# Rows beyond 128 of two expert blocks turned as one tile of 128 rows, and other short operands padded to 128

## The chip, the cores and the metric

One core of a Trainium2 chip runs the whole program. Its engines are TensorE (PE in the profile, with its weight loads shown apart as PEld), VectorE (DVE), ScalarE (ACT), GpSimd (POOL) and SyncE (SP), which here only issues transfers. The metric is the device time of one execution in microseconds (us). Three runs stand for the kernel before, and one more execution was profiled.

## What is computed

One layer of a hybrid trunk over 1024 tokens of width 1024: an mLSTM mixer, a residual layer norm, a mixture of 16 experts of which each token takes two, a second residual layer norm, and a gated embedding. The part around the change is the router and the experts:

```python
t = x.reshape(-1, d)                                    # 1024 tokens
scores = jax.nn.softmax((t @ router_w), axis=-1)        # 16 experts
...
for e in range(N_EXPERTS):
    h = jax.nn.silu(t @ w_gate[e]) * (t @ w_up[e])      # 1024 -> 512
    y = y + gate[:, e:e + 1] * (h @ w_down[e])          # 512 -> 1024
```

`gate` is zero for all but two experts of a token. The kernel therefore gathers for each expert only the tokens that chose it.

## The kernel before, in words

All large products are made of float32 operands split into a high and a low part (`split`: ACT writes the high part, DVE or POOL subtracts it for the low part), so that one product is two or three matmuls that go into the same sum.

The stages follow each other. The mixer's projections and its recurrence come first. Then a loop over eight tiles of 128 tokens (`project`, `normed`, `logits`) projects the mixer's output, adds the residual and makes the router's sums. In `logits` a first product puts high and low sums into 32 rows (`pl[:32, :128]`), DVE copies them to the tile `lt` of 32 partitions, and a second matmul of `lt` with the stacked identity `st2` adds the two halves and turns them at once (L890). The tiles 6 and 7 of this loop, the choice of the experts (`select`) and the placing of the tokens lie around the first expert block.

Then come 16 expert blocks. The experts are ordered by their number of tokens; `rank` is the place in that order, and `ORDER` alternates ranks below 8 with ranks from 8 on. A block r turns its gathered rows (`tr_full`, tile `xt`), and makes gate, up and down products for up to 128 rows. An expert of rank below 8 (even r) has up to 64 rows more, the mini part: `locate(r)` gathers them on POOL's queue into `xgm`, `turn_mini` (`tr_mini`) turns them while block r-1's up product runs, and `first_mini` makes gate and up of them, with high and low part side by side as 128 columns of one stationary tile `xm`. `fold` adds the two halves, `gated` multiplies silu(gate) by up into the tile `sg`, `tr_mini` turns the result (`hm`) between the steps of the down product, and `mini_out` makes the down product.

`turned` is the helper in which all these transposes are recorded (L446): four matmuls against the identity into one PSUM tile, then a split. With `n=64` it reads 64 partitions:

```python
PE.transpose(pt[:, k, :n], src[:n, 128 * (q + k):128 * (q + k) + 128], ident[:n, :n])
```

Block 0 is handled apart: its transposes of `xgm` stand as a group of eight, its `hm` is turned at L1293, and `fill_table` then makes for all blocks the table `tab` of token numbers by 32 small matmuls (L1196).

From the tile 6 of the projection on, the order on PE, ACT, DVE and POOL is the order in which the code is written; before it only that of PE and SP is. `run(chain, also=...)` weaves the steps of one generator between those of another, and `tick` hands out the splits of the coming expert's weights (`wraw` to `whi` and `wlo`) at fixed steps of PE's work.

Of the kernel before, what the change touches and what calls it, by code (L numbers as in the profile page):

```python
# [24 lines left out]
D = 1024  # L25
# [20 lines left out]
def trunk(ctx, tc, io, out):  # L46
# [79 lines left out]
    with ExitStack() as pa:  # L126
# [315 lines left out]
        def turned(src, q, hi, lo, n=128):  # L442

            pt = ptr.tile([128, 4, 128], F32, name="tr")
            for k in range(4):
                PE.transpose(pt[:, k, :n], src[:n, 128 * (q + k):128 * (q + k) + 128], ident[:n, :n])  # L446
            split(hi, lo, pt[:, :, :n])

# [135 lines left out]

    def gather_x(idx, n):
        xg = mt([128, D], F32, name="xg" if n == 128 else "xgm")
        G.indirect_dma_start(out=xg[:n], out_offset=None, in_=x1_d,
                             in_offset=bass.IndirectOffsetOnAxis(ap=idx[:n, :1], axis=0))
        return xg
# [11 lines left out]

    def tr_mini(res, src, nk, name):

        dst = mt([128, nk, 128], F32R, name=name, bufs=1)
        res.append(dst)
        for q in range(0, nk, 4):
            turned(src, q, dst[:, q:q + 4, :64], dst[:, q:q + 4, 64:], 64)
            yield

# [25 lines left out]

    def first_mini(res, x, w, name, late=False):
        ps = pmm.tile([128, 512], F32, name="mm")
        for k in range(ND):
            wh, wl = use(w[k // 4])
            product(ps, [(x[0][:, k], wh[:, k % 4]), (x[0][:, k], wl[:, k % 4])], k == 0, k == ND - 1)  # L640
            if k == ND - 1:
                if late:
                    yield
                dst = mt([64, DE], F32, name=name, bufs=1)
                fold(ps, dst)
                res.append(dst)
            yield
# [76 lines left out]

    FETCH, IDX, X, XM, WG, WU, WD = ({} for _ in range(7))
    mini = lambda i: ORDER[i] < NMINI
# [23 lines left out]
    def locate(r):  # L750

        e = ORDER[r]
        X[r] = gather_x(tab[:, 0, e:e + 1], 128)
        if mini(r):
            XM[r] = gather_x(tab[:, 1, e:e + 1], 64)

# [4 lines left out]
    def turn_mini(r):  # L761
        rows, XM[r] = XM[r], []
        return tr_mini(XM[r], rows, ND, "xm")

# [29 lines left out]
    with ExitStack() as pb_:  # L794
# [83 lines left out]
        def logits(t, bank=None):  # L878
# [102 lines left out]
        for t in range(NT - 1):  # L981
# [48 lines left out]
            if t < NT - 2:  # L1030
# [88 lines left out]
    with pe_:  # L1119
        PIECES[2] = [early, pe_.enter_context(pool("moew5", reuse_waits="tile"))]  # L1120
        home(pe_.enter_context(pool("moex", reuse_waits="tile")), "xg")
        home(pm_.enter_context(pool("moem", reuse_waits="tile")), "xm hm gs us fold e")
        last = NE - 1
        first_slot = lambda i: 128 * ORDER[i] + 64 * min(ORDER[i], NMINI)
# [65 lines left out]
        def fill_table():  # L1190

            pi = pix.tile([128, 512], F32, name="pi")
            for j, (a, b) in enumerate(((0, 128), (128, 192))):
                for k in range(2):
                    for c in range(NT):
                        PE.matmul(pi[:b - a, 32 * j:32 * j + 32], em[:, k, c, a:b], ids[:, k, c],  # L1196
                                  start=k + c == 0, stop=k + c == NT)
            idf = mt([128, 2, 2, NE], F32, name="idf", bufs=1)
            for j, n in enumerate((128, 64)):
                V.tensor_copy(idf[:n, j], pi[:n, 32 * j:32 * j + 32])  # L1200
                tt(tab[:n, j], idf[:n, j, 0], idf[:n, j, 1], op=ALU.add)

        V.tensor_copy(flat(prefs), prefp)
# [56 lines left out]
        ids = mt([128, 2, NT, 2, NE], BF, name="ids", tag="ht")  # L1260
        gm, chain = part(first_mini, XM[0], WG[0], "gs")
        run(chain, 5)
# [8 lines left out]
        splits(1)  # L1271
        um, chain = part(first_mini, XM[0], WU[0], "us", True)
        run(chain, 6)
# [8 lines left out]
        run(chain)  # L1282
        sg = gated(sg, um[0], 64)
        hm = sg
        fetcher(2)
# [6 lines left out]
        for k in range(4):  # L1292
            PE.transpose(pt[:, k, :64], hm[:64, 128 * k:128 * k + 128], ident[:64, :64])  # L1293
        hm32 = mt([128, NF, 128], F32, name="hm32", tag="hm", bufs=1)
# [73 lines left out]
        for r in range(1, NE):  # L1368
# [22 lines left out]
            if mini(r):  # L1391
                sg = silu(gm[0], 64)
                um, chain = part(first_mini, XM[r], WU[r], "us")
                run(chain)
                sg = gated(sg, um[0], 64)
            if r < last:
# [4 lines left out]
            if r < last:  # L1401
                g, chain = part(first_full, X[r + 1], WG[r + 1])
                if mini(r):
# [3 lines left out]
                    clock[1] = 1  # L1407
                    hm = sg
                    run(chain)
# [12 lines left out]
            if r < last and mini(r + 1):  # L1422
                gm, chain = part(first_mini, XM[r + 1], WG[r + 1], "gs")
                run(chain)
                if r + 2 < NE:
                    WG[r + 2] = fetch(r + 2, 0)
# [5 lines left out]
            if r == last:  # L1432
                WU[NE] = [queue_piece(raw_of(io["pgw"][i]), (2, D), 2, V) for i in range(2)]
                g2 = mt([128, D], F32, name="g2", tag="xgm")
# [44 lines left out]
        with tc.If(n_over > 0), tc.For_i(0, n_over):  # L1479
# [32 lines left out]
            V.tensor_copy(svb, sv)  # L1512
            e2 = mt([128, 2, NT, 128], BF, name="e2", tag="xgm")
            for k in range(2):
# [165 lines left out]
def _layout(x, p, ln1_g, ln1_b, ln2_g, ln2_b, mlstm_w_in, mlstm_conv, mlstm_gate_b, mlstm_norm_g,  # L1680
# [41 lines left out]
    d["pgw"] = c(ple_w_gate)[0].reshape(4, 2, 128, D).transpose(0, 2, 1, 3).reshape(4, 128, 2 * D)  # L1722
    d["st2"] = np.concatenate([np.eye(NE), np.eye(NE)])
    return {k: np.ascontiguousarray(v, dtype=np.float32) for k, v in d.items()}
# [15 lines left out]
```

## Time and profile before

| | |
|---|---|
| three runs | 978.39, 982.37, 984.08 us (median 982.37) |
| the profiled execution, its own time | 979.86 us |
| its span, first to last instruction | 978.2 us |
| PE busy | 959.8 us, 98% of the span |
| DVE, ACT, POOL busy | 655.0, 540.5, 249.4 us (67%, 55%, 25%) |

The span lies 1.66 us inside the profiled execution's own time. A busy PE is a PE with some matmul under way; matmuls overlap, so what one costs is read from the distance between starts. The three runs lie 5.7 us apart, which is 0.6% of the time.

### The profile page before, as it was taken

How to read it: one execution, taken by the hardware profiler on the slowest of the kernel's cores; microseconds unless marked ns; L12 is line 12 of the kernel's file. 1: busy time of each engine (PE TensorE's matmuls, PEld its weight loads, DVE VectorE, ACT ScalarE, POOL GpSimd, SP SyncE). 2: the span in 40 equal slices, each digit the busy share in tenths (PEclk: the TensorE clock that was granted, in tenths of full speed). 3: DMA queues.
4: the chain of work that ended last, by engine and by line, in shares of the span. 5: the costliest groups of instructions: out<-in, count | busy, mean ns of one | idle time of the engine just before them, and what ended most of it. 6: DMA issues, size and time to landing. Idle time of an engine off the chain costs nothing. (4 is left out here: it accounts for less than half of the span.)

```text
span 978.2 us, 14851 instructions
## 1 busy us (share of the span) xinstructions
PE 959.8 (98%) x5468; PEld 810.2 (83%) x5468; DVE 655.0 (67%) x1218; ACT 540.5 (55%) x902; POOL 249.4 (25%) x246
## 2 busy tenths in 40 slices
PE   7999999999999999998999999999999999999998
PEld 5989989899999888877668787878787878778887
DVE  5657656372443177789758779776767676688882
ACT  6336556454464255444358767676767576654441
POOL 0001212021000121111224442424242423233531
PEclk9999999999999999999999999999999999999999
DMA  8116921213336465612788988988989897764531
GB/s 314 64 51 250 331 82 55 75 49 92 97 104 202 157 237 211 234 51 104 256 297 318 329 325 293 335 332 291 335 290 341 315 347 297 271 239 147 173 108 65
DMA packets 51395, 207.03 MB, mean 212 GB/s; under 512 B 6892, under 2 KB 15724, under 8 KB 38264
## 3 DMA queue, kind: packets, MB, share of 16 engines
q1 hardware_dynamic: 43640, 182.48, 52.0%
q0 software_dynamic: 5968, 22.55, 6.9%
q10 hardware_dynamic: 1712, 1.03, 0.3%
q8 instruction: 44, 0.72, 0.3%
q14 instruction: 31, 0.25, 0.1%
HBM read 170.35 MB, written 35.68 MB: 211 GB/s over the span
## 5 line engine op out<-in xcount | busy, mean ns | idle before, releaser
L515 DVE TENSOR_TENSOR wlo<-wraw,whi 128x1024 fp32r<-128x1024 f32 x150 | 206.0, 1409 | 25.2 <-ACT whi L514 24.2
L514 ACT ACTIVATE whi<-wraw 128x1024 fp32r<-128x1024 f32 x194 | 195.1, 1051 | 9.1 <-DMA wraw<-eu 4.6
L63 PE MATMUL mm<-whi,xt 128*128 128x512 f32 (+1 forms) x528 | 168.4, 390 | 0.0
L515 POOL TENSOR_TENSOR wlo<-wraw,whi 128x1024 fp32r<-128x1024 f32 x44 | 108.8, 2481 | 224.4 <-ACT whi L514 224.3
L63 PE MATMUL mm<-wl,xh 128*128 128x256 f32 (+1 forms) x512 | 145.8, 285 | 0.0
L63 PE MATMUL mm<-wh,xh 128*128 128x256 f32 (+1 forms) x512 | 145.5, 284 | 0.0
L63 PE MATMUL mm<-wh,xl 128*128 128x256 f32 (+1 forms) x512 | 145.2, 284 | 0.0
L63 PEld LDWEIGHTS mm<-whi,xt 128*128 128x128 f32 x528 | 97.0, 188 | 21.7 <-issue 1.2
L63 PE MATMUL mm<-wlo,xt 128*128 128x512 f32 (+1 forms) x264 | 99.8, 387 | 0.9 <-DVE wlo L515 0.5
L63 PEld LDWEIGHTS mm<-wh,xh 128*128 128x128 f32 x512 | 96.8, 189 | 0.2 <-ACT sg L250 0.2
L63 PEld LDWEIGHTS mm<-wl,xh 128*128 128x128 f32 x512 | 96.8, 189 | 0.1
L63 PEld LDWEIGHTS mm<-wh,xl 128*128 128x128 f32 x512 | 96.7, 189 | 0.0
L63 PE MATMUL mm<-woh,yt 128*128 128x512 f32 x256 | 89.5, 408 | 0.3 <-ACT yt L57 0.3
L63 PE MATMUL mm<-whi,ht 128*128 128x512 f32 x240 | 86.3, 408 | 0.0
L63 PE MATMUL mm<-whi,x2t 128*128 128x512 f32 (+1 forms) x272 | 84.4, 385 | 0.0
L58 DVE TENSOR_TENSOR wl<-wr,wh 128x1024 fp32r<-128x1024 f32 (+2 forms) x26 | 29.7, 1145 | 45.4 <-ACT wh L57 45.0
L63 PEld LDWEIGHTS mm<-whi,x2t 128*128 128x128 f32 x272 | 50.1, 188 | 10.1
L63 PEld LDWEIGHTS mm<-wlo,xt 128*128 128x128 f32 x264 | 48.7, 188 | 11.0 <-DVE wlo L515 1.2
L63 PE MATMUL mm<-xh,wh 128*128 128x512 f32 x128 | 50.7, 405 | 6.9 <-ACT xh L57 6.9
L63 PEld LDWEIGHTS mm<-woh,yt 128*128 128x128 f32 x256 | 48.0, 188 | 10.7 <-ACT yt L57 0.5
L63 PEld LDWEIGHTS mm<-whi,ht 128*128 128x128 f32 x240 | 45.0, 188 | 10.6 <-DVE ht L58 0.8
L63 PE MATMUL mm<-wlo,x2t 128*128 128x512 f32 (+1 forms) x136 | 52.0, 382 | 0.0
(382 smaller groups left out, 1965.6 us busy)
## 6 DMA issues: line engine op xcount, KB each, us to landing
wraw<-eg SPq DMA_DIRECT2D x32, 1024.0 KB, 6.8
wraw<-ed SPq DMA_DIRECT2D x32, 1024.0 KB, 6.3
wraw<-eu SPq DMA_DIRECT2D x30, 1024.0 KB, 6.8
y_d<-zt SPq DMA_DIRECT2D x16, 512.0 KB, 5.6
y_d<-yo SPq DMA_DIRECT2D x14, 512.0 KB, 7.3
num_d<-nb SPq DMA_DIRECT2D x32, 128.0 KB, 1.8
wr<-wo SPq DMA_DIRECT2D x8, 512.0 KB, 4.5
sig_d<-sg SPq DMA_DIRECT2D x32, 128.0 KB, 1.8
```

The costliest lines, as they stand in the source:

```text
L58: (eng or V).tensor_tensor(lo, src, f32(hi), op=ALU.subtract)
L63: PE.matmul(ps, a, b, start=start and i == 0, stop=stop and i == n - 1)
L514: S.activation(hi[:, c], raw[:, c], AF.Copy)
L515: e.tensor_tensor(lo[:, c], raw[:, c], f32(hi)[:, c], op=ALU.subtract)
```

## The change

Mini rows of two blocks are gathered and turned together. Rows of block r (r = 2, 6, 10, 14) stand in partitions 0 to 63 of one `xgm` tile and rows of block r+2 in partitions 64 to 127 (for r = 14 the upper half holds rows that nothing uses); `tr_pair` turns them by 128-row transposes into one `xm` tile for both. `xgm` has one buffer now, and block 0 uses a first tile whose upper half is filled with zeros. The gated mini rows go into one fixed tile `us`, whose upper half is zeroed once, and are turned with 128 rows. `lt` becomes two fixed tiles of 128 partitions, zeroed but for the first 32, and `st2` has 128 rows. `fill_table` gets a third group of 16 matmuls, and one more addition on DVE, that put the table's rows for block r+2 into partitions 64 to 127.

```diff
@@ turned
             for k in range(4):
-                PE.transpose(pt[:, k, :n], src[:n, 128 * (q + k):128 * (q + k) + 128], ident[:n, :n])
-            split(hi, lo, pt[:, :, :n])
+                PE.transpose(pt[:, k], src[:, 128 * (q + k):128 * (q + k) + 128], ident)
+            split(hi, lo, pt[:, :, :n] if hi.ndim == 3 else pt.rearrange("p k (m t) -> p k m t", m=2))
...
-    def gather_x(idx, n):
-        xg = mt([128, D], F32, name="xg" if n == 128 else "xgm")
+    FIRST = []
+
+    def gather_x(idx, n, name="xg", **kw):
+        xg = FIRST.pop() if n == 64 else mt([128, D], F32, name=name, **kw)
...
+    def tr_pair(res, src):
+
+
+        dst = mt([128, ND, 2, 2, 64], F32R, name="xm", bufs=1)
+        res += [dst[:, :, i].rearrange("p k h t -> p k (h t)") for i in range(2)]
+        for q in range(0, ND, 4):
+            turned(src, q, *[dst[:, q:q + 4, :, i] for i in range(2)])
+            yield
...
-        if mini(r):
-            XM[r] = gather_x(tab[:, 1, e:e + 1], 64)
+        if r % 4 == 2:
+            XM[r] = gather_x(tab[:, 1, e:e + 1], 128, "xgm", bufs=1)
...
     def turn_mini(r):
-        rows, XM[r] = XM[r], []
-        return tr_mini(XM[r], rows, ND, "xm")
+
+        if r % 4 == 2 or r == 0:
+            pair = []
+            for j in range(2):
+                XMP[r + 2 * j] = pair, j
+            return tr_pair(pair, XM[r])
+        return iter(())
...
-        st2 = sp.tile([32, NE], F32, name="st2", bufs=1)
+        st2 = sp.tile([128, NE], F32, name="st2", bufs=1)
...
+        LT = [sp.tile([128, 128], F32, name=f"lt{i}", bufs=1) for i in range(2)]
+        for lt in LT:
+            G.memset(lt, 0.0)
...
             with tc.high_priority(offset=200):
-                lt = sp.tile([32, 128], F32, name="lt", bufs=2)
-                V.tensor_copy(lt, pl[:32, :128])
-            yield
-            PE.matmul(pl[:, 256:256 + NE], lt, st2, start=True, stop=True)
+                V.tensor_copy(LT[t % 2][:32], pl[:32, :128])
+            yield
+            PE.matmul(pl[:, 256:256 + NE], LT[t % 2], st2, start=True, stop=True)
...
+        FIRST.append(mt([128, D], F32, name="xgm", bufs=1))
+        G.memset(FIRST[0][64:], 0.0)
...
+        US = mt([128, DE], F32, name="us", bufs=1)
+        G.memset(US[64:], 0.0)
...
-            for j, (a, b) in enumerate(((0, 128), (128, 192))):
+            for j, a, b in (0, 0, 128), (1, 64, 192), (1, 128, 192):
...
+            tt(tab[64:, 1, :NE - 1], idf[64:, 1, 0, 1:], idf[64:, 1, 1, 1:], op=ALU.add)
...
-                sg = gated(sg, um[0], 64)
+                gated(US, sg, 64)
...
-                hmt, c2 = part(tr_mini, hm, NF, "hm")
+                hmt, c2 = part(tr_mini, US, "hm")
```

Three places in the order of instructions show it. The first is PE in the up product of block 3, where before the mini rows of block 4 (`xgm`) were turned in two groups of four between the matmuls of `xt`. Before:

```order
L63 MATMUL mm<-whi,xt_6349 128x512
L446 MATMUL tr<-cm,xgm 128x64 x4
L63 MATMUL mm<-whi,xt_6348 128x512
L63 MATMUL mm<-wlo,xt_6348 128x512
L63 MATMUL mm<-whi,xt_6349 128x512
L63 MATMUL mm<-whi,xt_6348 128x512
L63 MATMUL mm<-wlo,xt_6348 128x512
L63 MATMUL mm<-whi,xt_6349 128x512
L446 MATMUL tr<-cm,xgm 128x64 x4
L63 MATMUL mm<-whi,xt_6348 128x512
```

And the same place in the change:

```order
L63 MATMUL mm<-whi,xt_6364 128x512
L63 MATMUL mm<-whi,xt_6363 128x512
L63 MATMUL mm<-wlo,xt_6363 128x512
L63 MATMUL mm<-whi,xt_6364 128x512
L63 MATMUL mm<-whi,xt_6363 128x512
L63 MATMUL mm<-wlo,xt_6363 128x512
L63 MATMUL mm<-whi,xt_6364 128x512
L63 MATMUL mm<-whi,xt_6363 128x512
```

Both groups are gone, since block 4's rows were turned with those of block 2; blocks 8 and 12 lose theirs likewise, and the groups of blocks 2, 6, 10 and 14 stay where they were as transposes with 128 rows.

The second place is PE in the down product of block 2, where the gated mini rows are turned (`sg` before, `us` now). Before:

```order
L63 MATMUL mm<-wlo,ht 128x512
L63 MATMUL mm<-whi,ht 128x512
L446 MATMUL tr<-cm,sg 128x64 x4
L63 MATMUL mm<-whi,ht 128x512
L63 MATMUL mm<-wlo,ht 128x512
```

And in the change:

```order
L63 MATMUL mm<-wlo,ht 128x512
L63 MATMUL mm<-whi,ht 128x512
L446 MATMUL tr<-cm,us 128x128 x4
L63 MATMUL mm<-whi,ht 128x512
L63 MATMUL mm<-wlo,ht 128x512
```

Nothing moves here; the four transposes read 128 partitions in place of 64.

The third place is POOL from the projection to the first mini gather (`nm` is the mixer's output of a tile, the two `wlo` are weight splits of block 0, and `xgm` with `idx` is the gather of block 0's mini rows). Before:

```order
L468 TENSOR_TENSOR nm<-nm,sgm 128x1024 x8
L971 DMA xg_5504<-x_d,idx 128x1024
L534 TENSOR_TENSOR wlo<-wraw,whi 128x1024 x2
L587 DMA xgm<-x_d,idx 64x1024
L587 DMA xg<-x_d,idx 128x1024
```

And in the change:

```order
L468 TENSOR_TENSOR nm<-nm,sgm 128x1024
L832 MEMSET lt_4327 128x128
L832 MEMSET lt_4328 128x128
L468 TENSOR_TENSOR nm<-nm,sgm 128x1024 x7
L992 DMA xg_5502<-x_d,idx 128x1024
L1076 MEMSET xgm 64x1024
L534 TENSOR_TENSOR wlo<-wraw,whi 128x1024 x2
L1147 MEMSET us 64x512
L589 DMA xgm<-x_d,idx 64x1024
```

Four memsets stand in POOL's queue that were not there, one of them ahead of the two weight splits and one ahead of the gather.

## Rows read from the trace of the kernel before

**Rows 1.** Busy time by stage: us, each engine's busy us, clock, DMA share, GB/s
```profile
core 0: us, PE busy (x) PEld busy (x) DVE busy (x) ACT busy (x) POOL busy (x), PEclk, DMA share, GB/s
345.00:432.00 87.00, 87.00 (x495) 71.09 (x494) 70.18 (x251) 43.51 (x74) 14.56 (x6) 1.00 0.56 205
448.00:475.00 27.00, 23.66 (x126) 15.80 (x125) 22.36 (x80) 8.96 (x14) 5.64 (x3) 0.94 0.26 95
...
524.00:573.00 49.00, 49.00 (x231) 39.36 (x230) 37.99 (x42) 35.41 (x48) 23.84 (x12) 1.00 0.91 340
```

**Rows 2.** Waits of PE: who waited for whom, us in total, times, longest
```profile
PE mm L63 <- ACT xh L57: 6.9, 2, 5.8
...
PE mm L63 <- DVE wlo L515: 0.5, 1, 0.5
```

**Rows 3.** Timeline of PE around a group with 64 rows: start us, us, instruction
```profile
552.64 0.39 PE L63 MATMUL mm<-whi,xt 128*128 128x512 f32 x1
552.96 0.46 PE L446 MATMUL tr<-cm,xgm 64*128 64x64 f32 x4
...
553.69 0.39 PE L63 MATMUL mm<-wlo,xt 128*128 128x512 f32 x1
```

**Rows 4.** Timeline of PE around a group with 128 rows
```profile
590.57 0.39 PE L63 MATMUL mm<-whi,ht 128*128 128x512 f32 x1
590.80 0.60 PE L446 MATMUL tr<-cm,xg 128*128 128x128 f32 x4
...
591.47 0.39 PE L63 MATMUL mm<-wlo,ht 128*128 128x512 f32 x1
```

**Rows 5.** Timeline of PE in the projection, before and around the matmuls of lt
```profile
368.18 0.39 PE L63 MATMUL mm<-wol,yt 128*128 128x512 f32 x1
...
368.87 0.39 PE L63 MATMUL mm<-wol,yt 128*128 128x512 f32 x1
369.11 0.39 PE L63 MATMUL mm<-woh,yt 128*128 128x512 f32 x1
...
369.87 0.39 PE L890 MATMUL pi<-st,lt 32*128 32x16 f32 x2
...
370.52 0.40 PE L63 MATMUL mm<-wol,yt 128*128 128x512 f32 x1
```

**Rows 6.** Timeline of PE around a short float32 product with 128 rows
```profile
331.98 0.39 PE L63 MATMUL mm<-wol,yt 128*128 128x512 f32 x1
332.21 0.30 PE L818 MATMUL pi<-cs,ones 128*128 128x32 f32 x2
...
333.03 0.39 PE L63 MATMUL mm<-wol,yt 128*128 128x512 f32 x1
```

**Rows 7.** Timeline of PE: transposes of block 0, the table's matmuls, eight transposes
```profile
472.55 0.71 PE L446 MATMUL tr<-cm,xgm 64*128 64x64 f32 x8
...
481.84 1.18 PE L1196 MATMUL pi<-ids,e 128*128 128x32 bf16 x32
...
483.51 1.03 PE L446 MATMUL tr<-cm,xg 128*128 128x128 f32 x8
```

**Rows 8.** Timeline of POOL, then of DVE, around the router's last sums
```profile
448.59 4.74 POOL L534 TENSOR_TENSOR wlo<-wraw,whi 128x1024 fp32r<-128x1024 f32 x2 [8.79 <-ACT whi L530]
...
451.02 2.35 DVE L866 SCALAR_TENSOR_TENSOR shift<-cs,mv 128x16 f32<-128x16 f32 x1
```

**Rows 9.** Timeline of DVE, then of POOL, around a memset of POOL
```profile
86.97 1.22 DVE L58 TENSOR_TENSOR wl<-wr,wh 128x1024 fp32r<-128x1024 f32 x1
...
87.11 0.96 POOL L389 MEMSET zt<- 128x1024 f32 x1 [2.31 <-DVE wt L324]
```

**Rows 10.** Timeline of DVE, then of PE, at block 2's mini rows
```profile
512.53 0.42 DVE L58 TENSOR_TENSOR xm<-tr,xm 128x256 fp32r<-128x256 f32 x1 [1.56 <-ACT xm L57]
...
513.17 0.48 PE L63 MATMUL mm<-whi,xm 128*128 128x512 f32 x1
```

**Rows 11.** A mini gather's issue on POOL; DMA issues with median us to landing
```profile
530.86 1.91 POOL L587 DMA_INDIRECT xgm<-x_d,tab  x1 [0.30 <-issue]
...
xgm<-x_d,tab POOLq DMA_INDIRECT x7, 11.6
```

**Rows 12.** The stretch of low clock, columns as in the first group
```profile
466.00:470.00 4.00, 4.00 (x14) 1.88 (x13) 3.61 (x17) 0.38 (x1) 0.90 (x1) 0.57 0.20 62
```

More of the change, by code (lines that the diff above doesn't have):

```diff
@@ L600, in tr_full, with tr_mini @@
             yield
-    def tr_mini(res, src, nk, name):
-        dst = mt([128, nk, 128], F32R, name=name, bufs=1)
+    def tr_pair(res, src):
[4 more added lines that the diff above has]
+            yield
+    def tr_mini(res, src, name):
+        dst = mt([128, NF, 128], F32R, name=name, bufs=1)
         res.append(dst)
-        for q in range(0, nk, 4):
-            turned(src, q, dst[:, q:q + 4, :64], dst[:, q:q + 4, 64:], 64)
-            yield
+        turned(src, 0, dst[:, :, :64], dst[:, :, 64:], 64)
+        yield
     def first_full(res, x, w, ps=None):
@@ L634, in first_halves, with first_mini @@
                 yield
-    def first_mini(res, x, w, name, late=False):
+    def first_mini(res, x, w, dst, late=False):
         ps = pmm.tile([128, 512], F32, name="mm")
@@ L643, in first_mini @@
                     yield
-                dst = mt([64, DE], F32, name=name, bufs=1)
-                fold(ps, dst)
+                dst = mt([64, DE], F32, name=dst, bufs=1) if dst == "gs" else dst
+                fold(ps, dst[:64])
                 res.append(dst)
@@ L723, in carve @@
         return v
-    FETCH, IDX, X, XM, WG, WU, WD = ({} for _ in range(7))
+    FETCH, X, XM, XMP, WG, WU, WD = ({} for _ in range(7))
     mini = lambda i: ORDER[i] < NMINI
@@ L761, in turn_mini, with xm @@
     def turn_mini(r):
-        rows, XM[r] = XM[r], []
-        return tr_mini(XM[r], rows, ND, "xm")
+        if r % 4 == 2 or r == 0:
[4 more added lines that the diff above has]
+        return iter(())
+    def xm(r):
+        pair, j = XMP[r]
+        return [pair[j]]
     def raw_of(src):
@@ L1198, in fill_table @@
             idf = mt([128, 2, 2, NE], F32, name="idf", bufs=1)
-            for j, n in enumerate((128, 64)):
-                V.tensor_copy(idf[:n, j], pi[:n, 32 * j:32 * j + 32])
+            for j in range(2):
+                V.tensor_copy(idf[:, j], pi[:, 32 * j:32 * j + 32])
+                n = 128 >> j
                 tt(tab[:n, j], idf[:n, j, 0], idf[:n, j, 1], op=ALU.add)
+            tt(tab[64:, 1, :NE - 1], idf[64:, 1, 0, 1:], idf[64:, 1, 1, 1:], op=ALU.add)
         V.tensor_copy(flat(prefs), prefp)
@@ L1260, in trunk @@
         ids = mt([128, 2, NT, 2, NE], BF, name="ids", tag="ht")
-        gm, chain = part(first_mini, XM[0], WG[0], "gs")
+        gm, chain = part(first_mini, xm(0), WG[0], "gs")
         run(chain, 5)
@@ L1271, in trunk @@
         splits(1)
-        um, chain = part(first_mini, XM[0], WU[0], "us", True)
+        um, chain = part(first_mini, xm(0), WU[0], US, True)
         run(chain, 6)
@@ L1282, in trunk @@
         run(chain)
-        sg = gated(sg, um[0], 64)
-        hm = sg
+        gated(US, sg, 64)
         fetcher(2)
@@ L1292, in trunk @@
         for k in range(4):
-            PE.transpose(pt[:, k, :64], hm[:64, 128 * k:128 * k + 128], ident[:64, :64])
+            PE.transpose(pt[:, k], US[:, 128 * k:128 * k + 128], ident)
         hm32 = mt([128, NF, 128], F32, name="hm32", tag="hm", bufs=1)
@@ L1392, in trunk @@
                 sg = silu(gm[0], 64)
-                um, chain = part(first_mini, XM[r], WU[r], "us")
+                um, chain = part(first_mini, xm(r), WU[r], US)
                 run(chain)
-                sg = gated(sg, um[0], 64)
+                gated(US, sg, 64)
             if r < last:
@@ L1407, in trunk @@
                     clock[1] = 1
-                    hm = sg
                     run(chain)
@@ L1422, in trunk @@
             if r < last and mini(r + 1):
-                gm, chain = part(first_mini, XM[r + 1], WG[r + 1], "gs")
+                gm, chain = part(first_mini, xm(r + 1), WG[r + 1], "gs")
                 run(chain)
@@ L1433, in trunk @@
                 WU[NE] = [queue_piece(raw_of(io["pgw"][i]), (2, D), 2, V) for i in range(2)]
-                g2 = mt([128, D], F32, name="g2", tag="xgm")
+                g2 = mt([128, D], F32, name="g2", tag="xgm", bufs=1)
                 b2 = mt([128, D], F32, name="b2", tag="ht")
@@ L1512, in trunk @@
             V.tensor_copy(svb, sv)
-            e2 = mt([128, 2, NT, 128], BF, name="e2", tag="xgm")
+            e2 = mt([128, 2, NT, 128], BF, name="e2", tag="xt0")
             for k in range(2):
@@ L1722, in _layout @@
     d["pgw"] = c(ple_w_gate)[0].reshape(4, 2, 128, D).transpose(0, 2, 1, 3).reshape(4, 128, 2 * D)
-    d["st2"] = np.concatenate([np.eye(NE), np.eye(NE)])
+    d["st2"] = np.concatenate([np.eye(NE), np.eye(NE), np.zeros((128 - 2 * NE, NE))])
     return {k: np.ascontiguousarray(v, dtype=np.float32) for k, v in d.items()}
```

## Prediction

> **What bounds the kernel now.** I read the busy time by stage first. In the projection PE is busy for 87.00 of 87.00 us, and in a stretch of two expert blocks for 49.00 of 49.00, while DVE has 37.99 of those 49, ACT 35.41 and POOL 23.84 [rows 1]. Only the stretch in between, where the tokens are placed, leaves PE idle: 23.66 of 27.00 us, with DVE at 22.36 [rows 1]. The waits of PE come next. The longest entry of the list, 6.9 us, is the kernel's first load, and the only entry that the weights of the expert blocks cause is a single 0.5 us [rows 2]. So in the projection and in the blocks the time is what PE needs to pass its instructions through, and an instruction that costs PE less there moves all that follows. In the placing stage PE waits for DVE, and what PE saves just ahead of that wait is lost.
>
> As PE is always busy, busy time prices nothing. I price a group by the distance from the start of the product ahead of it to the start of the second product behind it, less two ordinary products. An ordinary 512-column product takes 0.23 us: three lie between 368.18 and 368.87 [rows 5]. I go to the second product behind because the first one's own step is often lengthened by the group.
>
> **The mini rows' transposes.** A group of four with 64 rows: 553.69 - 552.64 = 1.05, less 0.46, is 0.59 us [rows 3]. A group of four with 128 rows, at the same kind of place: 591.47 - 590.57 = 0.90, less 0.46, is 0.44 us [rows 4]. The group that turns more data is the cheaper one. Where the 0.59 goes can be seen: the first transpose starts 0.32 us behind the product ahead (552.64 to 552.96) where the 128-row one starts 0.23 behind (590.57 to 590.80), and the rest is lost on the way out. The transposes themselves are the cheaper ones with 64 rows: eight take 0.71 and four 0.46, so each more costs 0.06; with 128 rows eight take 1.03 and four 0.60, so 0.11 [rows 3, 4, 7]. So 64-row work costs little in itself and about 0.3 us for going in and out.
>
> [...]
>
> Blocks 2 to 14 have seven times two such groups, 14 x 0.59 = 8.26 us; now there are four times two with 128 rows, 8 x 0.44 = 3.52: **-4.74**. The gated rows of the same seven blocks are one group each, 0.59 before (they stand between products of the same size) and 0.44 now: 7 x 0.15 = **-1.05**. Block 0's eight transposes stay eight: 0.59 + 4 x 0.06 = 0.83 before, 0.44 + 4 x 0.11 = 0.88 after, **+0.05**; its gated rows are followed by a wait for ACT in any case, and I put them at nothing.
>
> **The router's sums.** With four transposes and the two matmuls of lt the distance is 370.52 - 369.11 = 1.41, less 0.46, is 0.95, of which the transposes have 0.44: the pair costs 0.51 us [rows 4, 5]. No row shows it with 128 partitions. The nearest is the product of `cs` with `ones`, also float32, two matmuls, a 128-column stationary tile and few columns: 333.03 - 331.98 = 1.05, less three products of 0.23, is 0.36 [rows 6]. The lower bound is two steps of 0.11, as transposes show them: 0.22. The upper is the present 0.51. I take 0.36, the same kind of instruction. It happens eight times, but the last two stand just ahead of the placing stage, where DVE's next step (`shift`) takes 2.35 us and ends with POOL's two weight splits (451.02 + 2.35 = 453.37 against 448.59 + 4.74 = 453.33) [rows 8]. That stage starts from POOL, not from PE, so six count: 6 x 0.15 = **-0.90** (bounds 0 and -1.74).
>
> **What is added.** The table's 32 matmuls take 1.18 us [rows 7]; 16 more cost at most half of it, **+0.59**, in a stretch where PE is not waiting. DVE's one more addition over 15 columns hides in the time that PE needs for these. The evictions of `xm` become half as many and twice as wide. DVE's second one for block 2 ends at 512.95, and the first product that reads `xm` starts at 513.17 [rows 10]; a wider one, at most twice 0.42 us, makes that product at most 0.2 to 0.4 us late, once. I take 0 and keep +0.4. In the later blocks a whole gate product lies between.
>
> POOL's four memsets: the widest that the trace has, 128 x 1024, takes 0.96 us, and DVE's subtraction beside it takes 1.22, no longer than others of its size [rows 9]. The one of `xgm` is ahead of the weight splits, and POOL idled 8.79 us ahead of those [rows 8]; the one of `us` is ahead of block 0's mini gather, behind splits that end at 453.33, with a gather that comes in the placing stage's second half. The two of `lt` are an eighth of that size, in a projection stage where POOL has 14.56 of 87 us [rows 1]. All at 0; if a memset held DVE up as the splits do, +0.96 for the one in the placing stage.
>
> The gathers fall from seven of 64 rows to four of 128. One is issued at 530.86 and its rows are turned from 552.96 on, 22 us later, while landing takes 11.6 [rows 3, 11]. Cost 0.
>
> **Sum.** -4.74 - 1.05 + 0.05 - 0.90 + 0.59 = **-6.05 us**. Bounds of the unknown prices: from -3.8 (lt gains nothing, `xm` late by 0.4, a memset that costs 0.96) to -6.9 (lt at 0.22). The profiled execution's own time is 979.86, which gives 973.8; the median of the three runs, 982.37, is 2.5 us above it, and from there it is 976.3. I forecast **975.0**, between them.
>
> [...]
>
> **The rivals.**
> *Columns alone.* If what costs in a 64-row group is not the number of rows, and the way in and out stays, the padded transposes only stream more. Then with 0.06 and 0.11 each: `xm` 56 x 0.06 = 3.36 becomes 32 x 0.11 = 3.52, block 0 +0.40, gated rows 32 x 0.05 = +1.60, table +0.59, lt 0: +2.8, and 982.7 from the own time, 985.2 from the median. [...] Chance 0.06.
> *Given back.* PE saves what I say, and waits take part of it: `xm` late (+0.4), a second stretch at the lower clock (+1.7). That leaves -4.0: 975.9 to 978.4, within the 0.5%. For it: DVE works 37.99 of 49 us, so a block gets little slack back. Against it: PE waits nowhere in the blocks. Chance 0.18.
> *A late gather, slower.* A gather of 128 rows has twice the data and one buffer. If it landed later than 22 us after its issue, PE would stand still in front of each pair. The price is the excess times four; to end over 0.5% slower it must pay back 6.05 and 4.9 more, 2.7 us for each pair, so landing at about 25 us against 11.6 now. It would give 987 or more. Against it: the gathers of whole blocks have 128 rows and PE waits for none of them [rows 2]. Chance 0.04.
> *The forecast* has 0.72.
>
> **How the numbers follow.** A difference of 0.5%, 4.9 us, is about what a measurement of this kernel tells from no change, since three runs of it lie 5.7 us apart. From 982.37 that is 977.5. The forecast lies below it (0.72); the first two rivals lie within, the first near the edge, so that I put 0.05 of it there and 0.01 to slower: 0.23 the same, and 0.05 slower with the late gather. The range goes from 970.5 (own time, cheap lt, no stretch of low clock) to 980.0 (a little under half-way from "given back" at 978.4 to no change).
>
> **What will show it.** A step of a group of four 128-row transposes at 0.44 us in the places of `xm` and `hm`; no transposes of `xgm` in blocks 3, 7 and 11; lt's pair at 0.2 to 0.4; the stretch between the same transposes of two blocks with and without a pair shorter by 1.2 + 0.15 and 0.3 + 0.15 us. The prediction is wrong if the 128-row groups cost 0.59 too, if PE's waits gain entries for `xm` or `xgm`, or if DVE's steps of the placing stage start later, against the end of the projection, than now.

## The result, and the profile after

The changed kernel takes 975.65 us (median of six runs, 975.38 to 977.04) where the kernel before takes 982.29 (six runs beside it, 978.39 to 984.08). The ratio is 0.9944, with a 95% interval from 0.9931 to 0.9958: 5.5 us faster by the ratio, while the medians lie 6.6 us apart. Measured once more later it was 975.92 against 981.99, ratio 0.9946 (0.9927 to 0.9964). The forecast was 975.0, faster by over 0.5%. The interval holds that bound, so the sign is certain and the size is at the edge of it. The profiled execution took 977.04, with a span of 975.4 us. One of the twelve executions of the run e3 below took 1916.2 us at a granted clock of 1.000 and is left out of its median and its ratio; it was not profiled, so why it took twice the time stays open.

The groups first, on PE's timeline (start us, us, instruction). A group of the paired `xgm`, where [rows 3] stood:

```profile
602.14 0.39 PE L63 MATMUL mm<-whi,xt 128*128 128x512 f32 x1
602.37 0.60 PE L446 MATMUL tr<-cm,xgm 128*128 128x128 f32 x4
...
603.04 0.40 PE L63 MATMUL mm<-wlo,xt 128*128 128x512 f32 x1
```

603.04 - 602.14 = 0.90, less two products of 0.23, is 0.44 us, as forecast. The same reading at the pair of lt, in the place of [rows 5]:

```profile
369.99 0.40 PE L63 MATMUL mm<-woh,yt 128*128 128x512 f32 x1
370.23 0.60 PE L446 MATMUL tr<-cm,nm 128*128 128x128 f32 x4
370.66 0.29 PE L911 MATMUL pi<-st,lt 128*128 128x16 f32 x2
...
371.12 0.40 PE L63 MATMUL mm<-wol,yt 128*128 128x512 f32 x1
```

371.12 - 369.99 = 1.13, less 0.46 and less the transposes' 0.44, is 0.23: the pair costs as two transposes do. Before it cost 0.51, and I had taken 0.36.

So lt gives more than I said, but the projection does not get shorter by it. By stage, with the columns of [rows 1], and a line for the low clock that answers to [rows 12]:

```profile
345.00:432.00 87.00, 86.43 (x495) 71.02 (x495) 72.85 (x246) 43.77 (x75) 14.49 (x6) 1.00 0.56 206
448.00:475.00 27.00, 23.50 (x122) 16.02 (x121) 22.46 (x79) 8.75 (x13) 6.21 (x4) 0.87 0.22 79
524.00:573.00 49.00, 49.00 (x231) 40.26 (x230) 38.09 (x42) 36.56 (x48) 24.11 (x10) 1.00 0.91 350
465.00:472.00 7.00, 6.53 (x18) 2.83 (x17) 5.36 (x25) 0.77 (x2) 0.94 (x1) 0.51 0.24 81
```

PE now idles in the projection (86.43 of 87 us, where it had 87.00). Around 465 us the granted clock is 0.51 over seven us, and 0.50 in each us from 466 to 471: 7 x 0.49 / 0.5 = 6.9 us at 0.50, against 4.00 x 0.43 / 0.5 = 3.4 before [rows 12], where it is 0.50 from 467 to 469. Two products of block 0's down product take 2.07 us there (468.14) and 1.02 behind it at 1.00 (475.51). So about half of that time is lost, and I estimate 3.5 x 0.5, about 1.7 us more than before in this execution. The list of PE's waits has entries that [rows 2] did not have:

```profile
PE mm L63 <- DVE ht L58: 0.4, 1, 0.4
...
PE pi L63 <- DVE xt L58: 0.4, 1, 0.4
```

The wait for xt is the projection's. `logits` makes eight products with RW, which read the high part of xt, and eight with RZ, which read the low part that DVE writes in two halves; the two kinds take turns, and the fifth RZ product is the first that reads the second half. Timelines of POOL, DVE and PE in one tile of the projection:

```profile
376.34 2.43 POOL L468 TENSOR_TENSOR nm<-nm,sgm 128x1024 f32<-128x1024 f32 x1 [11.37 <-ACT nm L467]
...
376.26 2.54 DVE L938 TENSOR_TENSOR sel<-sel 128x2 f32<-128x2 f32 x3
...
380.95 0.68 DVE L58 TENSOR_TENSOR xt<-tr,xt 128x512 fp32r<-128x512 f32 x1
...
381.38 0.22 PE L63 MATMUL pi<-xt,RW 128*32 128x128 f32 x1
381.68 0.25 PE L63 MATMUL pi<-xt,RZ 128*32 128x128 f32 x1
```

Three DVE operations on a few columns take 2.54 us together and end at 378.80, with POOL's product (376.34 + 2.43 = 378.77). All that DVE does behind them is late, by some 0.4 us: the next thing that it needs, ACT's `mv`, was written at 378.31 and is read at 378.72. RZ's fifth product then comes 0.30 behind RW's fifth (381.38 to 381.68) where such steps are 0.06, as they all are in these tiles before the change. In this execution four of the tiles show it, with steps of 0.29, 0.30, 0.29 and 0.58 us (the list above counts only what is left between overlapping matmuls). The first of the four can't be put down to `lt`: e4 below, with `lt` as before, has one of 0.30 at the same place.

Last, the table: 48 matmuls in place of the 32 of [rows 7].

```profile
484.06 1.57 PE L1221 MATMUL pi<-ids,e 128*128 128x32 bf16 x48
```

Read by equal products of both traces (start after less start before), the change stands at +1.12 us ahead of the projection (it came in the first 15 us: 0.33 are there at 10.6 us, behind a wait of 0.32 for `wh` while ACT waits 0.48 for its load, and the rest comes from 12.4 us on, where products start 0.43 us apart until 14.4, and before only until 12.4), +0.78 at 456 us, +2.22 at 480 (the clock), +2.67 at 500 (the table), -2.58 at 860 and -2.83 at the end. A second profile of the change (that of e9, span 971.6), in which the clock did not fall in the placing stage (1.00 from 465 to 475 us), reads 0.00, -0.06, -1.65, -1.22, -6.16 and -6.60 at the same places.

### The profile page after: what moved, and what is told of

It reads as the page before. It is cut to its first block, busy times and chain, and to the rows that moved or that the text cites. A ratio compares the mean times of both kernels' runs of the same rounds, so it can differ in the third digit from the quotient of the medians.

```text
span 975.4 us, 14816 instructions
## 1 busy us (share of the span) xinstructions
PE 955.4 (98%) x5460; PEld 812.6 (83%) x5460; DVE 661.7 (68%) x1213; ACT 540.8 (55%) x896; POOL 249.8 (26%) x247
```

## The experiments

Kernels of one set ran on one chip, beside runs of the kernel before: e1 to e4, e5 to e8, e9 to e12.

**e1: the router's sums alone.** The kernel before, with the edits of `lt` and `st2` only.

```diff
...
-                lt = sp.tile([32, 128], F32, name="lt", bufs=2)
-                V.tensor_copy(lt, pl[:32, :128])
+                V.tensor_copy(LT[t % 2][:32], pl[:32, :128])
...
```

> The kernel before with one part of the change: lt as two fixed zeroed tiles of 128 partitions and st2 with 128 rows. Theory (caught by DVE): lt's pair falls from 0.51 to 0.22 us, as the trace after the change shows, which would be 6 x 0.29 = 1.7 us, but PE then comes to the products that read xt before DVE has written its low part, DVE being held beside POOL's product in some tiles; the stretch of 72.4 us between the first transposes of nm of the first and the last tile of the projection gets shorter by 0.3 to 1.0 us only, with one or more new waits of PE for DVE's xt, and the whole run gets faster by 0.3 to 1.0 us. Rival (all is kept): that stretch is shorter by 1.4 to 1.7 us and the run by the same. Rival (prediction's size): pair at 0.36, stretch shorter by 0.9.

980.53 us against 981.08 (ratio 0.9996, 0.9984 to 1.0009): the time alone does not tell it from the kernel before. The trace does. The pair is at 0.22. The first transposes of nm in tiles 2 and 7, before and then in e1:

```profile
353.05 0.60 PE L446 MATMUL tr<-cm,nm 128*128 128x128 f32 x4
...
425.45 0.49 PE L446 MATMUL tr<-cm,nm 128*128 128x128 f32 x3
```

```profile
353.49 0.38 PE L446 MATMUL tr<-cm,nm 128*128 128x128 f32 x2
...
425.26 0.60 PE L446 MATMUL tr<-cm,nm 128*128 128x128 f32 x4
```

72.40 us become 71.77: of the 5 x 0.29 = 1.45 that the five pairs in between save, 0.63 are kept. Two tiles of the five are shorter by the full 0.29 (14.19 us in place of 14.46 to 14.50); the other three take 14.41 to 14.50, and in these RZ's fifth product stands 0.29, 0.26 and 0.32 behind RW's fifth. The theory holds. The rival that all is kept is out; my 0.15 a pair comes near to what was kept (0.13), but not for my reason.

**e2: the gated rows alone.** The kernel before, with the tile `us` of 128 rows.

```diff
...
-            turned(src, q, dst[:, q:q + 4, :64], dst[:, q:q + 4, 64:], 64)
+            turned(src, q, dst[:, q:q + 4, :64], dst[:, q:q + 4, 64:], 64, nk == NF)
...
-                sg = gated(sg, um[0], 64)
+                gated(US, sg, 64)
...
```

> The kernel before with one part of the change: the gated rows in one fixed tile of 128 rows, zeroed above row 64, and turned by transposes of 128 rows; one group of four in each of seven blocks. Theory (row count): a group falls from 0.59 to 0.44 us, 7 x 0.15 = 1.05 us less. Rival (columns alone): 32 x 0.05 = 1.6 us more, with groups at 0.59 + 4 x 0.05 = 0.79.

980.95 us against 981.08 (0.9994, 0.9980 to 1.0008). A difference of 1 us is inside this interval, so the time alone says only that it is not 1.6 us slower. The trace says the rest: the groups stand at 0.44 to 0.45 us, and from 500 to 860 us equal products gain 0.87, beside 7 x 0.15 forecast.

**e3: padded, not paired.** The kernel before, with `xgm` in two fixed tiles whose upper halves are zero, and as many transposes as before.

```diff
...
-        xg = mt([128, D], F32, name="xg" if n == 128 else "xgm")
+        xg = mt([128, D], F32, name="xg") if n == 128 else XGM[0]
+        if n == 64:
+            XGM.reverse()
...
-            turned(src, q, dst[:, q:q + 4, :64], dst[:, q:q + 4, 64:], 64)
+            turned(src, q, dst[:, q:q + 4, :64], dst[:, q:q + 4, 64:], 64, nk == ND)
...
```

> The kernel before with xgm in two fixed tiles whose upper halves are zeroed, turned by as many transposes as before, each of 128 rows in place of 64: nothing is paired. Theory (leaving and entering 128 rows is what costs): each of 14 groups falls from 0.59 to 0.44 us, -2.1 us, block 0 +0.05, so about 2 us faster. [...] Rival (only the halving counts): groups stay at 0.59, no change.

979.90 us against 981.08 (0.9983, 0.9966 to 1.0000). This is the run that decides between row count and columns, and it does so by its trace, since the interval just reaches no change. A group on PE's timeline of this kernel:

```profile
555.41 0.40 PE L63 MATMUL mm<-whi,xt 128*128 128x512 f32 x1
555.65 0.60 PE L447 MATMUL tr<-cm,xgm 128*128 128x128 f32 x4
...
556.32 0.40 PE L63 MATMUL mm<-wlo,xt 128*128 128x512 f32 x1
```

556.32 - 555.41 - 0.46 = 0.45 us: the group of as many transposes, each with twice the rows and twice the columns, is 0.14 cheaper. From 500 to 860 us equal products gain 1.8 us against before, beside 2.1 forecast. "Columns alone" would make each of the 64 transposes 0.05 dearer: a group at 0.59 + 4 x 0.05 = 0.79, and the kernel 3.2 us slower.

**e4: the pairs alone.** The change with `lt` and the gated rows' transposes put back.

```diff
-                PE.transpose(pt[:, k], src[:, 128 * (q + k):128 * (q + k) + 128], ident)
+                PE.transpose(pt[:, k, :n], src[:n, 128 * (q + k):128 * (q + k) + 128], ident[:n, :n])
...
```

> The change without its padding of the router's sums and of the gated rows: only the pairs of mini rows, and the table's 16 more matmuls. Theory: 14 groups at 0.59 become 8 at 0.44 (-4.74), block 0 +0.05, the table +0.59: 4.1 us faster. Rival (columns alone): 56 x 0.06 becomes 32 x 0.11, block 0 +0.4, table +0.59: 1.2 us slower. Rival (only the halving counts): 14 x 0.59 becomes 8 x 0.59, so -3.5 + 0.6 = 2.9 us faster.

977.28 us against 981.08: 3.8 us less by the medians, 3.5 by the ratio (0.9964, 0.9951 to 0.9978), beside 4.1 forecast. The pairs are two thirds of the change.

**e5: where the step lies.** The change, with the gated rows turned with another number of rows in each block.

```diff
-                PE.transpose(pt[:, k], src[:, 128 * (q + k):128 * (q + k) + 128], ident)
+                PE.transpose(pt[:, k, :m], src[:m, 128 * (q + k):128 * (q + k) + 128], ident[:m, :m])
...
+        ROWS = [64, 65, 96, 112, 120, 127, 128]
...
```

> The change with its gated rows turned with another number of rows (and as many columns) in each block: 64, 65, 96, 112, 120, 127 and 128 rows in blocks 2, 4, 6, 8, 10, 12 and 14. Theory (half of the array is a mode of its own): 64 rows 0.59 us a group, all others 0.44 or less (by the columns, down to 4 x 0.06 + about 0.05 at 65). Rival (any tile short of 128 rows pays): 0.59 or more for all but 128 rows. The whole time is that of the change within its scatter.

976.64 us in its one run. The groups cost 0.60, 0.31, 0.37, 0.41, 0.43, 0.44 and 0.44 us for 64, 65, 96, 112, 120, 127 and 128 rows. The first two, on PE's timeline:

```profile
542.59 0.40 PE L63 MATMUL mm<-whi,ht 128*128 128x512 f32 x1
542.91 0.46 PE L446 MATMUL tr<-cm,us 64*128 64x64 f32 x4
...
543.64 0.40 PE L63 MATMUL mm<-wlo,ht 128*128 128x512 f32 x1
```

```profile
590.11 0.39 PE L63 MATMUL mm<-whi,ht 128*128 128x512 f32 x1
590.35 0.41 PE L446 MATMUL tr<-cm,us 65*128 65x65 f32 x4
...
590.88 0.39 PE L63 MATMUL mm<-wlo,ht 128*128 128x512 f32 x1
```

One row more saves 0.29 us. It shows on the way in and out: the first transpose starts 0.24 behind the product ahead instead of 0.32, and the second product behind the group follows the last transposes sooner. From 65 rows on the price rises again; rows and columns grow together here, and in e12, where only the rows change, the price from 65 on stays the same, so it is the columns. So it is a step between 64 and 65 rows, not a price of each row that is missing; what TensorE does at this step no run shows. 65 rows would have been a better padding for `us` than 128.

**e6: filling PE's waits.** The change, with 24 transposes of the identity ahead of three waits of the placing stage (the same helper written out ahead of the product with `AB`).

```diff
...
+        def warm(n):
+            pt = ptr.tile([128, 4, 128], F32, name="tr")
+            for k in range(n):
+                PE.transpose(pt[:, k % 4], ident, ident)
...
         gate(0)
+        warm(12)
         turn32(0)
...
```

> The change with 24 transposes of the identity (8, 12 and 4, into a PSUM tile that nobody reads) put on PE ahead of three of its waits in the placing stage: for AB, for sg and for h. They take 24 x 0.11 = 2.6 us, and the waits there are 0.83, 0.27, 0.40, 1.46 and 0.47 us. Theory (the waits bring the clock down, and the clock explains most of what differs between executions): the granted clock between 465 and 475 us is 1.00 in place of 0.66, and the time falls by about 3.4 us, half of the 6.8 us at the lower level, to 972.2. Rival (the fall has another cause, or such short work does not count): clock and time as in the change, 975.7. Rival (they are in the way): the chain through DVE gets later by up to 1 us.

975.47 us against 982.26 (0.9928, 0.9910 to 0.9947): 0.2 less than the change by the medians, 1.6 by the ratios, whose intervals overlap, and not the 3.4 expected. Windows as in [rows 1], around the placing stage and around the wait for z ahead of the last stage:

```profile
465.00:475.00 10.00, 9.96 (x48) 5.22 (x47) 7.88 (x35) 2.74 (x6) 1.07 (x2) 1.00 0.51 181
866.00:880.00 14.00, 10.87 (x45) 8.58 (x44) 12.01 (x17) 6.04 (x11) 3.98 (x5) 0.88 0.67 240
```

The clock stays at 1.00 in the first, and equal products, which come 0.4 us sooner than in the profile of the change at 456 us, come 3.4 sooner at 475: 3.0 us are gained there. In this execution the gain was given back at the end: PE waited 3.1 us for z (1.8 in the profile of the change), behind that wait the clock fell (0.88), and at 876 us 0.4 is left.

**e7: POOL in pieces.** The change, with POOL's long operations beside the router cut to 256 columns.

```diff
-            G.tensor_tensor(nm, nm, sg, op=ALU.mult)
+            for h in range(H):
+                G.tensor_tensor(nm[:, h], nm[:, h], sg[:, h], op=ALU.mult)
...
-            eng.tensor_tensor(lo[:, c], raw[:, c], f32(hi)[:, c], op=ALU.subtract)
+            for b in range(c.start, c.stop, 256 if eng is G else 1024):
+                d = slice(b, b + (256 if eng is G else 1024))
+                eng.tensor_tensor(lo[:, d], raw[:, d], f32(hi)[:, d], op=ALU.subtract)
```

> The change with POOL's product of nm and sgm in four pieces of 256 columns, and POOL's weight splits of block 0 in pieces of 256. Theory (one DVE operation that reads two SBUF tiles is held until POOL's whole operation ends): no DVE operation there lasts over 1 us, the waits of PE for xt behind RW's first product (0.29, 0.30, 0.29 and 0.58 us in place of 0.06) go, the stretch from the first transposes of nm of tile 2 to those of tile 7 falls from 72.07 to about 70.9 us, and shift no longer takes 2.3 us; -1.2 us in the projection and 0 to -2 in the placing stage. Rival (POOL's pieces follow each other so closely that DVE is held as before, or POOL gets slower): no change, or POOL's product late and PE waiting for nm.

975.27 us against 982.26 (0.9934, 0.9917 to 0.9951): not to be told from the change. What was expected of DVE came about in part. Near 376 us its six operations on `sel` take 1.99 us together where they took 2.76 in the change (and 0.52 before it, where POOL's product starts 0.37 behind them), and `shift` behind the last sums [rows 8] takes 0.67 in place of 2.35. POOL's splits now take 6.61 us in place of 4.74:

```profile
449.08 6.61 POOL L537 TENSOR_TENSOR wlo<-wraw,whi 128x256 fp32r<-128x256 f32 x8 [6.26 <-ACT whi L531]
...
451.25 0.67 DVE L891 SCALAR_TENSOR_TENSOR shift<-cs,mv 128x16 f32<-128x16 f32 x1
```

But PE gains little. Against the change the product with `AB` comes 1.23 us sooner, 0.86 of it from the placing stage, and the stretch from tile 2 to tile 7 takes 71.81 us in place of 72.07, where 70.9 was expected. Three of the four waits for xt are gone, one new one of 0.30 came, and the longest stayed. ACT, DVE, then PE, at that place:

```profile
403.69 1.71 ACT L467 ACTIVATE nm<-nm,spc 128x256 f32<-128x256 f32 x4 [2.17 <-DMA nm<-num_d]
...
407.53 0.16 DVE L888 RECIPROCAL mv<-mv 128x1 f32<-128x1 f32 x1 [2.45 <-ACT mv L886]
...
408.34 1.28 DVE L897 SCALAR_TENSOR_TENSOR zres<-zres,mv,g 128x1024 f32<-128x1024 f32 x1
...
409.75 0.68 DVE L58 TENSOR_TENSOR xt<-tr,xt 128x512 fp32r<-128x512 f32 x1
...
409.92 0.22 PE L63 MATMUL pi<-xt,RW 128*32 128x128 f32 x1
410.49 0.25 PE L63 MATMUL pi<-xt,RZ 128*32 128x128 f32 x1 [0.35 <-DVE xt L58]
```

And ACT and DVE one tile earlier, where PE does not wait:

```profile
388.84 1.71 ACT L467 ACTIVATE nm<-nm,spc 128x256 f32<-128x256 f32 x4 [1.52 <-DMA nm<-num_d]
...
392.67 0.16 DVE L888 RECIPROCAL mv<-mv 128x1 f32<-128x1 f32 x1 [0.69 <-ACT mv L886]
```

POOL holds nothing up here. ACT waits for the load of `nm` and starts 14.85 us after the tile before, while the products with RW come after 14.21; what ACT does in its order, up to `mv`, is 0.64 late with it. DVE waits 2.45 us for `mv`, and then works through its own order, in which the normalising of `zres` (1.28 us) stands ahead of the part of xt that PE needs. The order is the same one tile earlier, and there it is in time. So POOL is one cause and the load of `nm`, by way of ACT and of DVE's order, another; which of them shows differs from tile to tile. That a sooner load would end the wait was not tried.

**e8: fill and pieces together.** The diffs of e6 and e7, both.

> The change with the fill and the pieces together. Theory: the two gains add, -3.4 - 1.2 us, about 971. Rival (the pieces move the waits away from where the fill stands, so that it is in the way): no better than the better of the two.

973.46 us against 982.26 (0.9911, 0.9891 to 0.9932), 2.2 under the change's first median (3.2 by the ratios) with intervals that overlap, and not the 971 expected. In its profile the clock is 1.00 from 465 to 475 us and 0.88 from 866 to 880, as in e6.

**e9: the change once more**, for a comparison on the chip of e10 and e11.

> The change itself once more, beside the next two on the same chip. Its median as before, 975.7 us within 1, with a mean granted clock of about 0.996.

975.92 us against 981.99 (0.9946, 0.9927 to 0.9964).

**e10: the best version.** e8, with 65 rows for the gated rows of seven blocks, and 16 more transposes of the identity ahead of the last stage's first ones.

```diff
...
-        turned(src, 0, dst[:, :, :64], dst[:, :, 64:], 64)
+        turned(src, 0, dst[:, :, :64], dst[:, :, 64:], 64, 65)
...
+        for k in range(16):
+            PE.transpose(pt[:, k % 4], ident, ident)
         turn2(0, 0)
...
```

> Fill and pieces together, the gated rows of seven blocks turned with 65 rows and 65 columns (0.31 us a group where 128 takes 0.44), and 16 more transposes of the identity ahead of the wait for z near 870 us, which in the profiles of the fill brought the clock down for 2 to 3 us. Theory: 7 x 0.13 = 0.9 us less in the blocks and 1.6 us less at the end than fill and pieces alone, about 971; every profiled stretch behind 465 us at a clock of 1.00. Rival (the fall of the clock at the end has another cause): 972.5.

972.69 us against 981.99 (0.9913, 0.9893 to 0.9933). That is 3.2 us under the change's median on the same chip, six runs each (971.44 to 974.98, and 973.34 to 977.51). It is not the 971 expected but close to the rival's 972.5, though the clock did what the theory said. The windows of e6, now:

```profile
465.00:475.00 10.00, 10.00 (x50) 5.78 (x50) 7.87 (x34) 2.58 (x5) 1.91 (x2) 1.00 0.60 218
866.00:880.00 14.00, 13.06 (x65) 10.57 (x64) 12.94 (x16) 6.98 (x12) 2.45 (x3) 1.00 0.57 203
```

The mean granted clock of all its six executions is 0.999 or 1.000; of the change's twelve, one is at 1.000 and the others at 0.995 to 0.998. The groups of 65 rows cost 0.31 us, as in e5. Of the gain in time I put over half down to the clock: between the second profile of the change and this one, both without a fall, lie 1.85 us at 860 us and 0.7 at the end, or 1.4 without the 0.7 that this execution came later out of its first 20 us. What is lost between is the wait for z: its last operation on DVE, behind the gathers of `y`, ends only 0.61 sooner (867.16 in place of 867.77).

**e11: products ahead of the first load.** e10, with ten bfloat16 products over zeros while PE waits for its first load.

```diff
...
+        for _ in range(10):
+            PE.matmul(pz, wz[:, :128], wz, start=True, stop=True)
...
```

> The same with ten bfloat16 products of 512 columns over zeros ahead of the kernel's first product, in the 5.6 us in which PE waits for its first load. Theory: the first products, which now take 0.43 us each until 14 us, take 0.23 us sooner; the loads set the pace up to 12 us, so the gain is 0.5 to 1.5 us. Rival (the loads set the pace of the whole start): no change.

972.66 us against 981.99 (0.9902, 0.9883 to 0.9921), the same as e10. The start of PE's timeline:

```profile
1.34 4.10 PE L184 MATMUL mm<-wz 128*128 128x512 bf16 x10 [1.34 <-DVE epsc L380]
5.90 0.49 PE L63 MATMUL mm<-xh,wh 128*128 128x512 f32 x1 [0.46 <-ACT xh L57]
...
9.00 0.79 PE L63 MATMUL mm<-xh,wh 128*128 128x512 f32 x1 [1.65 <-ACT xh L57]
...
12.73 0.63 PE L63 MATMUL mm<-xl,wh 128*128 128x512 f32 x1
```

The first product takes 0.49 us where it had 0.79; at 9 us, behind a wait of 1.65 us for `xh`, a product takes 0.79 again. Up to 12 us equal products come 0.05 us later than in e10. PE waits there in both, 1.65 and 0.21 us here and 1.41 in e10, for ACT's `xh` and `wh`, for whose loads ACT itself waits (2.70 and 0.48 us in the profile of the change), as the rival says. Behind it they come later still, 0.70 at 16 us: in e10 a product takes 0.39 from 14 us on, and here only from 15. So the products ahead moved the stretch of slow products and did not take it away. What makes them slow the granted clock does not show: over the first 15 us it is 1.00 in e10 and 0.78 here.

**e12: the step for lt.** The change, with 128, 32, 33, 64, 65, 96, 127 and 128 partitions in lt's pair, by tile.

```diff
-            PE.matmul(pl[:, 256:256 + NE], LT[t % 2], st2, start=True, stop=True)
+            n = (128, 32, 33, 64, 65, 96, 127, 128)[t]
+            PE.matmul(pl[:, 256:256 + NE], LT[t % 2][:n], st2[:n], start=True, stop=True)
```

> The change with another number of partitions in lt's pair for each tile of the projection: 128, 32, 33, 64, 65, 96, 127 and 128 for tiles 0 to 7, with the same 128 columns of lt and 16 of st2. Theory (what the gated rows showed holds for lt): a group of four transposes and the pair takes 0.96 us at 32, 33 and 64 partitions and 0.66 from 65 on. Rival (32 partitions are a mode apart from 64): 33 and 64 differ from 32. Rival (any count below 128 is dear): only 128 at 0.66.

976.45 us in its one run. With the four transposes the pair takes 0.96, 0.96 and 0.95 us at 32, 33 and 64 partitions, and 0.67 at 65, 96 and 128 (tiles 0 to 5; those of 127 and the last of 128 stand between other products and can't be read so). The tiles of 64 and 65:

```profile
399.77 0.39 PE L63 MATMUL mm<-woh,yt 128*128 128x512 f32 x1
...
400.53 0.39 PE L912 MATMUL pi<-st,lt 64*128 64x16 f32 x2
...
401.18 0.40 PE L63 MATMUL mm<-wol,yt 128*128 128x512 f32 x1
```

```profile
414.26 0.39 PE L63 MATMUL mm<-woh,yt 128*128 128x512 f32 x1
...
414.93 0.29 PE L912 MATMUL pi<-st,lt 65*128 65x16 f32 x2
...
415.39 0.40 PE L63 MATMUL mm<-wol,yt 128*128 128x512 f32 x1
```

1.41 and 1.13 us between the outer products. The columns are the same in both, so here the row count alone makes the 0.28. In this execution PE waits 1.72 us for xt in the tile of 32 partitions; ACT had waited 2.20 us for the load of `nm` ahead of it, as at the place shown for e7.

## Why the prediction was right, point by point

**The price of 64 rows** was right, and it was the step on which all rested. Groups at 0.44 with 128 rows are what the changed kernel shows in the places of the 0.59, and e3, e5 and e12 show that it is the row count. In e5 the groups of 65 to 128 rows get dearer with their columns (0.31 to 0.44 us; an estimate from these two is 0.13 / (4 x 63), about 0.5 ns a column), and that of 64 rows, 0.60, does not fit them: a price by the columns alone would put it below the 0.31 of 65. So the rival made of such a price is out.

**The pairs and the gated rows** were forecast at -5.79 us. From 500 to 860 us the two profiles of the change give -5.25 and -4.94. Most of what is missing can be seen: the wait for `ht` in the list above, near 615 us, where DVE's low part comes after PE, a step of 0.83 us in both profiles that was 0.35 before. The second profile has one more, near 534 us, where DVE's `sg` comes after PE and a step of 0.44 stands in place of 0.23:

```profile
533.70 0.39 PE L63 MATMUL mm<-whi,xt 128*128 128x512 f32 x1
...
534.14 0.66 PE L446 MATMUL tr<-cm,sg 128*128 128x128 f32 x4
```

The last 0.1 us or so of either profile I can't place. I had written that PE waits nowhere in the blocks, which was so before the change, and gave a 0.18 chance to "given back" by other waits; such waits came, and they are small. What e4 timed for pairs and table, 3.8 us, agrees with 4.1.

**The table** was forecast at +0.59 and measures +0.45 and +0.43 (480 to 500 us).

**The router's sums** are the term that went wrong twice, with errors of opposite sign. The pair was mis-sized: 0.22 us, the lower bound of my range, and not 0.36, so that six pairs would have been -1.74. I took a product with `ones` of 32 columns [rows 6] for the nearest kind. And "only the last two tiles count for nothing" failed: I looked for what waits behind PE only at the placing stage, where [rows 8] show DVE's `shift` end with POOL's splits (453.37 and 453.33). POOL has a long product in every tile of the projection too (2.41 to 2.48 us near 376 and 390), and in some a DVE operation lasts until its end: one took 2.40 us near 390 us before the change, two take 2.40 near 376 and 391 in it. With PE 0.29 us faster a tile, DVE's part of xt, which had just been in time, is late (a step of 0.30 us in place of 0.06). e1 keeps 0.63 us of 1.45 over five tiles, near the 0.75 that I had for five, which is luck; the change itself keeps 0.34 and 0.06 us up to 456 us, where I had 0.90. That DVE is held is read from the times alone: three operations on a few columns take 2.54 us and end at 378.80, with POOL's at 378.77, and with POOL's work in pieces of 256 columns (e7) `shift` takes 0.67 in place of 2.35. So e7 shows that it is one cause here, beside the load of `nm`; what in the two operations makes DVE wait was not shown.

**The clock** was no small print. "Given back" and the lower end of the range count a stretch of low clock at 1.7 us; this is an estimate, 4.00 x (1 - 0.57) from [rows 12], and no run times such a stretch by itself. What the runs showed in its place: at 0.50 were spent 3.4 us in the profile of before, 6.9 in the first of the change and none in the second, and e6, at 1.00 from 465 to 475 us where the change had 0.66, gained 3.0 us between 456 and 475 us.

**The late gather** did not come: PE has no wait for `xgm` or `xm`. Nor did the memsets hold DVE up at the end of the projection: from the first product of the last sums to `shift` it is 6.28 us before and 6.34 in the change.

**The sum**: from 500 us to the end -5.50 and -5.38, the table +0.45 and +0.43, from ahead of the projection to 456 us -0.34 and -0.06: -5.4 and -5.0 us by the two traces, without start and clock, where I had -6.05. The two timed comparisons give 5.5 and 5.3 us by their ratios, 6.6 and 6.1 by their medians. That the row count sets the price, on which the larger terms rest, was right; that the median, 975.65, lies only 0.65 us from 975.0 is in part luck, since that number was chosen between forecasts from two bases 2.5 us apart and with the clock an execution moves by as much (spans of 976.5 to 977.2 us before the change at 1.000, 979.5 to 981.3 at 0.996). The lower end of the range was also added up wrongly: own time, cheap lt and no stretch of low clock give 971.3, not 970.5.

## What to carry to other kernels

A short matmul or transpose between full ones is priced by the distance from the product ahead to the second product behind, and those that read 64 partitions or fewer here cost 0.3 us more than with 65: a group of four transposes 0.60 against 0.31 (e5), a pair with 32, 33 or 64 partitions 0.28 to 0.29 more (e12). Padding the partitions with zeros took that away, without halving anything; 65 were enough, and for the transposes, whose columns grow with them, cheaper than 128 (0.31 against 0.44). Where an engine that is always busy gets faster, look at each place where another engine had been just in time: e1 kept 0.63 of 1.45 us there. And where a stage leaves PE idle, compare the granted clock of several executions before crediting a microsecond or two to an edit: from 465 to 475 us it was 0.66 in one profile of the change and 1.00 in the other.

## What the hardware showed that I had not expected

The step between 64 and 65 rows: 0.60 and 0.31 us for a group of four transposes, 0.51 and 0.23 for a pair of float32 matmuls with 16 columns, and for that pair no step between 32 and 64.

How much of the scatter between executions is the clock: in 55 executions of the kernel before, the span is 976.5 to 977.2 us at a mean granted clock of 1.000 (3 of them), 977.5 to 979.4 at 0.998 (9), 979.5 to 981.3 at 0.996 (7); the 20 at 0.997 overlap with these, at 979.2 to 981.3. A line through all 55 falls by about 1 us for each 0.001 of the clock. Behind PE's waits in the placing stage the clock fell in some profiles and not in others. Of ten profiles without the fill (before, the change, e1 to e5, e7, e9, e12) eight have a granted clock of 0.66 to 0.83 between 465 and 475 us and two have 1.00, with the same waits; all four with the fill have 1.00. So in these profiles transposes of no use were enough to keep it up there, while a fall in the last stage came in two of the four (and in one of the ten, e2) and was gone in the two that fill that wait too.
